# Moving the conv gate columns of a hybrid conv/attention block into the attention stage

## The chip, the core and the metric

The kernel runs on one core of one Trainium2 chip. Time is device microseconds for one execution. Engines are named as in the profile: PE is TensorE (matmuls), PEld its weight loads, DVE is VectorE, ACT is ScalarE, POOL is GpSimd, SP is SyncE, which here only issues DMAs. TensorE's clock is granted at one of two levels, 1.2 or 2.4 GHz; the profile gives it as a share of full speed.

## What is computed

One decoder block on x of 1024 positions by 1024 channels, in fp32:

```
h    = rmsnorm(x, norm_in_g);   P = h @ w_in           # q, 3 x (k, v), branch gates, z_nsa, glu_in, z_conv, merge_g
o    = nsa_attention(...)                              # compressed, selected and window branches, 16 heads
y_nsa  = (o * silu(z_nsa)) @ w_nsa_proj
u    = a * sigmoid(b)                                  # glu_in = (a, b)
c    = silu(layernorm(causal_depthwise_conv31(u), conv_ln_g, conv_ln_b))
y_conv = (c * silu(z_conv)) @ w_conv_proj
g_conv, g_nsa = split(sigmoid(merge_g))
x    = x + (g_conv * y_conv + g_nsa * y_nsa) @ w_out;  out = rmsnorm(x, norm_f_g)
```

## The kernel before

Activations are kept transposed, channels on the 128 partitions and positions along the free axis. A matrix product in fp32 is made of three passes: every operand is split into a high and a low part, and high*high, high*low and low*high are summed in PSUM. `split_w` (line 104) does this for weights: `load_w` brings 4 row blocks of a 128-column strip (256 KB, two `raw` buffers), ScalarE rounds them (`wh`, line 109) and GpSimd takes the rest (`wl`, line 110 through the helper at line 69). A *column* below is one such strip of 128 output channels: 2 halves of 512 positions, 24 matmuls of 512 columns in each half (`mm_seq`, lines 113 to 123), 48 matmuls in all.

The stages, in program order:

- norm of x and transposes; `hT` holds the split h in SBUF, two halves.
- front projections by `project` (line 364): GLU columns, k, q, v. Beside them VectorE runs the depthwise convolution (31 taps, line 347), in pieces that `pump` hands out after each half column. The convolution's result is `cv`, 8 tiles of 128x1024.
- 8 columns of the NSA gate z_nsa (`C_ZN`): ScalarE sigmoid and a VectorE product (`zs`, lines 556, 557), stored to `ZD`.
- the layer norm of `cv` (lines 566 to 599), raised in priority: column sums by matmul with ones, eight subtractions of the mean (line 586), squares, sums on GpSimd (line 590), reciprocal root, eight products (line 594), silu.
- `EARLY` = 3 columns of the merge gates (`C_MG`): one ScalarE tanh each half, stored to `GD`.
- 8 columns of the conv gate z_conv (`C_ZC`, lines 609 to 618): sigmoid, two VectorE products, one of them with the normalised `cv`, stored to `YD`.
- attention in 8 steps of (group, pair of query blocks), order (0,0), (0,1), (1,0), (1,1), (0,2), (0,3), (1,2), (1,3), each with 8 heads. `select` loads q and does the compressed branch, `attend` the other two.
- beside attention, at lowest priority and through one PSUM bank (`fbank`), *filler* matmuls: first the 13 other merge gate columns (`merge_gates`), then the conv projection (`projections`, 8 columns, needs all of `YD`, and uses the memory of `hT`), then most of the NSA projection (`nsa_early`, 8 columns: the first half of positions whole, of the second half 12 matmuls each). `pace` ties the pieces of `nsa_early` to heads of the last two steps, as the earliest point at which they may be issued.
- after attention: the rest of the NSA projection and the output projection.

The order of instructions on each engine is not written by hand. A planner with a cost model simulates the program when it is built, takes the ready instruction with the highest priority and assigns memory; then each engine runs its fixed order. `tc.high_priority(offset=LOW)` pushes work behind everything else. A tile pool that is opened where another was closed may have to wait for that memory. In the kernel before, the pools of attention (`gp` for K, V and bias; `sp` for q; `ap`) are opened after the block that holds `cv`.

Of the kernel before, what the change touches and what calls it, by code (L numbers as in the profile page):

```python
# [16 lines left out]
P = 128  # L17
# [6 lines left out]
HG = 8  # L24
# [30 lines left out]
EARLY = 3  # L55
# [3 lines left out]
def hybrid_block(ctx, tc, x, norm_in_g, w_in, pos_ck, w_ck1, w_ck2, pos_cv, w_cv1, w_cv2,  # L59
# [13 lines left out]
    wp = ctx.enter_context(tc.tile_pool(name="wp", bufs=2))  # L73
    dram = ctx.enter_context(tc.tile_pool(name="dram", bufs=1, space=DRAM))
# [16 lines left out]
    MD = dram.tile([D, S], F32, name="MD")  # L91
    ND = dram.tile([2, D, HALF], F32, name="ND")
# [124 lines left out]

    with ExitStack() as c1:
# [14 lines left out]
        up = c1.enter_context(tc.tile_pool(name="up", bufs=1, reuse_waits="tile"))  # L233
# [90 lines left out]
        pc = c1.enter_context(tc.tile_pool(name="pc", bufs=1, reuse_waits="tile"))  # L324
        pv_ = c1.enter_context(tc.tile_pool(name="pcv", bufs=1, side="right", reuse_waits="tile"))
        st = c1.enter_context(tc.tile_pool(name="st", bufs=2, side="right", reuse_waits="tile"))
        cv = pv_.tile([P, KT, S], F32, name="cv")
        csum = pc.tile([P, S], F32, name="csum")
# [7 lines left out]
        def conv_pair(ct, us):  # L336
            def gen():
                accs = [pcc.tile([P, S], F32, tag="ca", name="ca", bufs=2) for _ in range(2)]
                for k in range(TAPS):
                    for e in range(2):  # L340
                        u, w = us[e][:, k:k + S], vec[:, ct + e, V_CW + k:V_CW + k + 1]
                        if k == 0:
                            nc.vector.tensor_scalar(accs[e], u, w, vec[:, ct + e, V_CB:V_CB + 1],
                                                    op0=ALU.mult, op1=ALU.add)
                        else:
                            dst = accs[e] if k < TAPS - 1 else cv[:, ct + e, :]
                            nc.vector.scalar_tensor_tensor(dst, u, w, accs[e], op0=ALU.mult, op1=ALU.add)  # L347
                        yield
                for e in range(2):
                    if ct + e == 1:  # L350
                        nc.gpsimd.tensor_tensor(csum, cv[:, 0, :], cv[:, 1, :], op=ALU.add)
                    elif ct + e > 1:
                        nc.gpsimd.tensor_tensor(csum, csum, cv[:, ct + e, :], op=ALU.add)
# [17 lines left out]
        def glu_pair(c0):  # L371
            us = []
            for ct in (c0, c0 + 1):
                u, sg = glu_buffers(st) if ct else first_glu
# [171 lines left out]

        nc.gpsimd.memset(bc[:, :, 0:56], 0.0)
        for h4 in range(0, NH, 4):
            tmp = st.tile([P, 4, 256], F32, tag="sg", name="tmp", bufs=2)
# [3 lines left out]
        for t in range(KT):  # L553
            def ev_zn(hf, ps):
                zs = st.tile([P, HALF], F32, tag="zs", name="zs", bufs=2)
# [4 lines left out]
            project(C_ZN + t * P, ev_zn)  # L560
        pump(10 ** 6)
        conv_stack.close()
        psums["ax"] = c1.enter_context(tc.tile_pool(name="pl", bufs=4, space=PSUM, side="right", reuse_waits="tile"))

        lnp = c1.enter_context(tc.tile_pool(name="lnp", bufs=1, reuse_waits="tile"))
        with tc.high_priority(offset=4 * AHEAD):
            mu = lnp.tile([P, S], F32, name="mu")
            def column_sums(total):
# [5 lines left out]
                for hf in range(2):  # L574
                    ps = aux()
# [9 lines left out]
            for k in range(KT):  # L585
                nc.vector.tensor_tensor(cv[:, k, :], cv[:, k, :], mu, op=ALU.subtract)
                sq = lnp.tile([P, S], F32, tag="sq", name="sq", bufs=2) if k else vsum
                nc.scalar.activation(sq, cv[:, k, :], AF.Square)
# [3 lines left out]
            for k in range(KT):  # L592
                sg = st.tile([P, S], F32, tag="sg", name="sg", bufs=2)
                nc.vector.tensor_tensor(cv[:, k, :], cv[:, k, :], rs, op=ALU.mult)
                nc.scalar.activation(sg, cv[:, k, :], AF.Sigmoid, scale=vec[:, k, V_LG:V_LG + 1],
                                     bias=vec[:, k, V_LB:V_LB + 1])
                nc.vector.tensor_scalar(cv[:, k, :], cv[:, k, :], vec[:, k, V_LG:V_LG + 1],
                                        vec[:, k, V_LB:V_LB + 1], op0=ALU.mult, op1=ALU.add)
                nc.gpsimd.tensor_tensor(cv[:, k, :], cv[:, k, :], sg, op=ALU.mult)

        for j in range(EARLY):
            def ev_mg(hf, ps, j=j):
                mg = st.tile([P, HALF], F32, tag="zs", name="mg", bufs=2)
                nc.scalar.activation(mg, ps, AF.Tanh, scale=0.5)
                nc.sync.dma_start(GD[j * P:(j + 1) * P, hf * HALF:(hf + 1) * HALF], mg)

            project(C_MG + j * P, ev_mg)
# [12 lines left out]
    pf = ctx.enter_context(tc.tile_pool(name="pf", bufs=1, space=PSUM, reuse_waits="tile"))  # L620
    ev = ctx.enter_context(tc.tile_pool(name="ev", bufs=3, reuse_waits="tile"))
# [31 lines left out]
    with ExitStack() as c3:  # L653
        psS = c3.enter_context(tc.tile_pool(name="psS", bufs=3, space=PSUM, side="right", reuse_waits="tile"))
        psT = c3.enter_context(tc.tile_pool(name="psT", bufs=3, space=PSUM, reuse_waits="tile"))
        psO = c3.enter_context(tc.tile_pool(name="psO", bufs=1, space=PSUM, reuse_waits="tile"))
        gp = c3.enter_context(tc.tile_pool(name="gp", bufs=1, reuse_waits="tile"))
# [3 lines left out]
        def merge_gates():  # L661
            cols = [w_in[:, C_MG + j * P:C_MG + (j + 1) * P] for j in range(EARLY, 2 * KT)]
            for n, hf, ps in ends_halved(cols, hT, fbank, (False, True)):
                j = EARLY + n
                sl = slice(hf * HALF, (hf + 1) * HALF)
# [3 lines left out]
                nc.sync.dma_start(GD[j * P:(j + 1) * P, sl], mg)  # L669

        with tc.high_priority(offset=LOW):
            merge_gates()

        K = [gp.tile([P, 2, S], F32R, name=f"k{j}") for j in range(2)]
        V = [gp.tile([P, NB, P], F32R, name=f"v{br}") for br in range(2)]
        BT, base, shared = {}, {}, {}

        def load_kv(g, half, slot):
            src_t, dst_t = slice(half * HALF, (half + 1) * HALF), slice(slot * HALF, (slot + 1) * HALF)
            for br in (1, 0):  # L680
                for part in range(2):
                    src = KD[br, part, g * DK:(g + 1) * DK, src_t]
                    for j in range(2):
                        r0 = (part ^ j) * DK
                        nc.sync.dma_start(f(K[j][r0:r0 + DK, br, dst_t]), src)
            for br in (1, 0):
                nc.sync.dma_start(f(V[br][:, 4 * slot:4 * slot + 4, :]),
                                  VD[g, br, src_t].rearrange("(c p) n -> p c n", p=P))
            base[g] = (slot - half) * 4

        def load_bt(g):
            BT[g] = []
            for h8 in range(HG):
# [417 lines left out]
```

## Time and profile before

| | |
|---|---|
| time, median of 3 runs | 1464.44 us (1464.18 to 1464.65) |
| profiled execution, its own time | 1461.95 us |
| its span, first to last instruction | 1460.2 us |
| mean granted TensorE clock | 0.988 |
| matmuls in flight (PE) | 1402.9 us, 96% of the span |
| VectorE busy | 1046.3 us, 72% |
| DMA moved | 171.16 MB |

The profile is one execution. Matmuls are pipelined, so the busy time of PE is the time in which at least one is in flight; it doesn't say how densely they follow each other. Durations of single matmuls overlap for the same reason. The time of an execution is a little longer than its span.

### The profile page before, as it was taken

To read this page: it belongs to the slowest core of one execution; us is meant where nothing else is said; L and a number is where in the kernel's file an instruction comes from. 1 tells how busy PE (TensorE), PEld (TensorE's weight loads), DVE (VectorE), ACT (ScalarE), POOL (GpSimd) and SP (SyncE) were. 2 spreads that over 40 slices of the span, in tenths; PEclk is the share of its full clock that TensorE was granted. 3 is DMA by queue.
4 is the path that set the end of the run, shared out by engine and by line. 5 is a ranking of instruction groups with operands and counts; after the bars stand their busy time and mean duration, and the time that the engine had idled before them with its cause. 6 is when DMAs were issued, how large, how long until landed. Compare 5 with 4: busy or idle time off the path is not lost.

```text
span 1460.2 us, 22837 instructions
## 1 busy us (share of the span) xinstructions
PE 1402.9 (96%) x7516; PEld 1203.8 (82%) x7516; DVE 1046.3 (72%) x2382; ACT 675.7 (46%) x1440; POOL 687.5 (47%) x793
## 2 busy tenths in 40 slices
PE   7999999999989999999999999999999899999997
PEld 6788888888868788778888788898799789898786
DVE  5699999999866522257665956766878988886732
ACT  6331112112144322256666675565567677775422
POOL 2323224233172822255545596455677477774211
PEclk8999999999999999999999999999999999999999
DMA  5243424345223733523333375322444223434732
GB/s 170 70 117 102 129 58 152 109 130 164 80 80 87 197 110 98 148 77 95 91 86 97 94 228 163 95 87 91 155 132 137 78 62 94 152 109 148 216 116 87
DMA packets 185711, 171.16 MB, mean 117 GB/s; under 512 B 12165, under 2 KB 146389, under 8 KB 185592
## 3 DMA queue, kind: packets, MB, share of 16 engines
q1 hardware_dynamic: 183528, 166.55, 38.2%
q10 hardware_dynamic: 2064, 3.15, 0.7%
q8 instruction: 60, 0.98, 0.3%
q14 instruction: 59, 0.48, 0.1%
HBM read 124.01 MB, written 48.78 MB: 118 GB/s over the span
## 4 chain that ended last, share of the span: by engine, by line
PE 80%; DVE 10%; issue 3%; DMA 2%; ACT 2%; POOL 1%; SPq 1%; ACTq 0%; DVEq 0%; POOLq 0%
PE mm L120 10%; PE mm L122 10%; PE mm L121 10%; PE sb L813 6%; PE tb L860 6%; PE fb L120 4%; PE fb L121 3%; PE fb L122 3%; PE ob L886 3%; PE ob L885 3%; PE fb L132 3%; PE fb L133 3%; PE fb L134 3%; PE eb L1044 2%; PE eb L1043 2%
## 5 line engine op out<-in xcount | busy, mean ns | idle before, releaser
L69 POOL TENSOR_TENSOR wl<-raw,wh 128x512 fp32r<-128x512 f32 x184 | 243.6, 1325 | 430.2 <-ACT wh L109 404.1
L120 PE MATMUL mm<-act,wh 128*128 128x512 f32 x720 | 284.5, 395 | 6.8 <-DVE zs L557 6.8
L347 DVE SCALAR_TENSOR_TENSOR ca<-u,vec,ca 128x1024 f32<-128x1024 f32 x232 | 284.0, 1281 | 0.8
L121 PE MATMUL mm<-act,wh 128*128 128x512 f32 x720 | 281.1, 391 | 0.0
L122 PE MATMUL mm<-act,wl 128*128 128x512 f32 x720 | 277.9, 391 | 0.2 <-POOL wl L69 0.2
L109 ACT ACTIVATE wh<-raw 128x512 fp32r<-128x512 f32 x184 | 115.5, 628 | 262.8 <-PE mm L121 179.6
L848 ACT ACTIVATE p<-p,ac 128x640 f32<-128x640 f32 (+7 forms) x256 | 187.5, 734 | 65.2 <-DVE ac L840 55.9
L853 POOL TENSOR_SCALAR p<-p,rcx,gates 128x640 f32<-128x640 f32 (+7 forms) x256 | 200.4, 794 | 10.6
L813 PE MATMUL sb<-k,q 128*128 128x384 f32 (+2 forms) x704 | 178.8, 352 | 6.1 <-DVE ac L840 6.0
L69 DVE TENSOR_TENSOR tl<-tb,th 128x512 fp32r<-128x512 f32 (+1 forms) x272 | 158.4, 591 | 29.5 <-ACT th L864 27.9
L860 PE MATMUL tb<-ident,p 128*128 128x128 f32 x1056 | 169.4, 274 | 5.6 <-DVE tl L69 2.4
L864 ACT ACTIVATE th<-tb 128x512 fp32r<-128x512 f32 (+1 forms) x272 | 136.0, 517 | 68.3 <-PE tb L860 59.2
L120 PEld LDWEIGHTS mm<-act,wh 128*128 128x128 f32 x720 | 135.5, 188 | 36.2 <-DVE zs L557 7.7
L122 PEld LDWEIGHTS mm<-act,wl 128*128 128x128 f32 x720 | 135.6, 188 | 29.3 <-POOL wl L69 0.6
L121 PEld LDWEIGHTS mm<-act,wh 128*128 128x128 f32 x720 | 135.7, 188 | 28.0
L860 PEld LDWEIGHTS tb<-ident,p 128*128 128x128 f32 x1056 | 125.9, 141 | 13.4 <-DVE tl L69 3.1
L813 PEld LDWEIGHTS sb<-k,q 128*128 128x128 f32 x704 | 114.4, 191 | 16.8 <-issue 3.8
L886 PE MATMUL ob<-tl,v 128*128 128x256 f32 x448 | 124.5, 298 | 3.9 <-DVE tl L69 3.4
L885 PE MATMUL ob<-th,v 128*128 128x256 f32 x448 | 124.8, 292 | 0.5 <-ACT th L864 0.4
L120 PE MATMUL fb<-act,wh 128*128 128x512 f32 x240 | 96.3, 401 | 0.7 <-ACT mg L668 0.6
L122 PE MATMUL fb<-act,wl 128*128 128x512 f32 x240 | 95.6, 398 | 0.0
L121 PE MATMUL fb<-act,wh 128*128 128x512 f32 x240 | 95.2, 397 | 0.0
(244 smaller groups left out, 2594.2 us busy)
## 6 DMA issues: line engine op xcount, KB each, us to landing
raw<-in_w_in_dram SPq DMA_DIRECT2D x128, 256.0 KB, 3.0
gt<-GD SPq DMA_DIRECT2D x40, 256.0 KB, 3.2
GD<-mg SPq DMA_DIRECT2D x32, 256.0 KB, 2.8
q<-QD SPq DMA_DIRECT2D x64, 128.0 KB, 3.2
raw<-in_w_nsa_proj_dram SPq DMA_DIRECT2D x32, 256.0 KB, 3.7
raw<-in_w_conv_proj_dram SPq DMA_DIRECT2D x24, 256.0 KB, 3.0
k<-KD SPq DMA_DIRECT2D x40, 128.0 KB, 3.2
xt<-in_x_dram SPq DMA_DIRECT2D x8, 512.0 KB, 6.1
```

Of the source, the lines that this page charges most:

```text
L69: eng.tensor_tensor(low, full, f(high), op=ALU.subtract)
L120: nc.tensor.matmul(ps, wh[:, k, :], mh[:, kk, :], start=(kk == 0), stop=False)
L121: nc.tensor.matmul(ps, wh[:, k, :], ml[:, kk, :], start=False, stop=False)
L122: nc.tensor.matmul(ps, wl[:, k, :], mh[:, kk, :], start=False, stop=(kk == KT - 1))
L347: nc.vector.scalar_tensor_tensor(dst, u, w, accs[e], op0=ALU.mult, op1=ALU.add)
L813: nc.tensor.matmul(s[:, 0:w], lhs, K[j][:, br, k0:k0 + w], start=(j == 0), stop=(j == 1))
L848: nc.scalar.activation(pt[:, 0:n], pt[:, 0:n], AF.Exp, bias=mn, scale=-1.0, accum_out=sm[:, b:b + 1])
L853: nc.gpsimd.tensor_scalar(pt[:, 0:n], pt[:, 0:n], rc[:, b:b + 1], gates[:, 2 * qp + b, gcol:gcol + 1], op0=ALU.mult, op1=ALU.mult)
L860: nc.tensor.transpose(tp[:, j * P:(j + 1) * P], src, ident)
L864: nc.scalar.activation(th, src, AF.Copy)
L885: nc.tensor.matmul(dst, lhs, th[:, sl], start=False, stop=False)
L886: last = nc.tensor.matmul(dst, lhs, tl[:, sl], start=False, stop=False)
```

## The change

Three things. (1) The eight conv gate columns leave the front and become filler in attention, at the head of the filler queue, ahead of the merge gates; `EARLY` goes from 3 to 6, so 10 merge gate columns are left to the filler in place of 13. The normalised conv result is stored to a new DRAM tensor `CD` (8 stores of 512 KB), and each half column of the gate loads its part back (16 loads of 256 KB). silu is computed as tanh with the factor 0.5 folded into the layer norm's scale and bias (`half_ln`), one VectorE instruction in place of two products, and the product with `ct` goes to GpSimd. (2) Ahead of the end of the convolution stand only two NSA gate columns; behind the layer norm come four merge gate columns, then the six other NSA gate columns, and two merge gate columns at lowest priority. (3) The pool of K, V and bias (`gp`) and the PSUM pools of attention are opened ahead of the layer norm, whose column sums use attention's PSUM tiles, and the first loads of K, V and bias are written right behind the layer norm. `cv` becomes eight tiles; the evacuation tiles of the front come from the pool `ev` with three buffers.

```diff
-EARLY = 3
+EARLY = 6
+    ev = ctx.enter_context(tc.tile_pool(name="ev", bufs=3, reuse_waits="tile"))
+    CD = dram.tile([D, S], F32, name="CD")
...
+        half_ln = vp_.tile([P, KT, 2], F32, name="half_ln")
...
-        cv = pv_.tile([P, KT, S], F32, name="cv")
+        cv = [pv_.tile([P, S], F32, name=f"cv{k}") for k in range(KT)]
...
+        nc.vector.tensor_scalar(half_ln, vec[:, :, V_LG:V_LG + 2], 0.5, None, op0=ALU.mult)
...
-        for t in range(KT):
+        def zn_col(t):
             def ev_zn(hf, ps):
-                zs = st.tile([P, HALF], F32, tag="zs", name="zs", bufs=2)
+                zs = ev.tile([P, HALF], F32, tag="ev", name="zs")
...
+        def gate_col(j):
+            def ev_mg(hf, ps):
+                mg = ev.tile([P, HALF], F32, tag="ev", name="mg")
+                nc.scalar.activation(mg, ps, AF.Tanh, scale=0.5)
+                nc.sync.dma_start(GD[j * P:(j + 1) * P, hf * HALF:(hf + 1) * HALF], mg)
+
+            project(C_MG + j * P, ev_mg)
+
+        for t in range(2):
+            zn_col(t)
         pump(10 ** 6)
         conv_stack.close()
-        psums["ax"] = c1.enter_context(tc.tile_pool(name="pl", bufs=4, space=PSUM, side="right", reuse_waits="tile"))
+        up_stack.close()
+        pf = ctx.enter_context(tc.tile_pool(name="pf", bufs=1, space=PSUM, side="right", reuse_waits="tile"))
+        psS = att.enter_context(tc.tile_pool(name="psS", bufs=3, space=PSUM, side="right", reuse_waits="tile"))
+        gp = att.enter_context(tc.tile_pool(name="gp", bufs=1, reuse_waits="tile"))
...
-                    ps = aux()
+                    ps = psS.tile([P, HALF], F32, tag="s", name="sb")
...
+                nc.vector.tensor_scalar(cv[k], cv[k], half_ln[:, k, 0:1], half_ln[:, k, 1:2],
+                                        op0=ALU.mult, op1=ALU.add)
+                nc.gpsimd.tensor_tensor(cv[k], cv[k], sg, op=ALU.mult)
+                nc.sync.dma_start(CD[k * P:(k + 1) * P, :], cv[k])
-        for j in range(EARLY):
...
-        for t in range(KT):
-            def ev_zc(hf, ps):
-                sl = slice(hf * HALF, (hf + 1) * HALF)
-                zs = st.tile([P, HALF], F32, tag="zs", name="zs", bufs=2)
-                nc.scalar.activation(zs, ps, AF.Sigmoid)
-                nc.vector.tensor_tensor(zs, ps, zs, op=ALU.mult)
-                nc.vector.tensor_tensor(zs, zs, cv[:, t, sl], op=ALU.mult)
-                nc.sync.dma_start(YD[t * P:(t + 1) * P, sl], zs)
-
-            project(C_ZC + t * P, ev_zc)
...
+        load_bt(0)
+        load_kv(0, 0, 0)
+        load_kv(1, 0, 1)
+        for j in range(4):
+            gate_col(j)
+        for t in range(2, KT):
+            zn_col(t)
+        with tc.high_priority(offset=LOW):
+            for j in range(4, EARLY):
+                gate_col(j)
...
-        def merge_gates():
...
+        def late_columns():
+            todo = [(C_ZC, t) for t in range(KT)] + [(C_MG, j) for j in range(EARLY, 2 * KT)]
+            cols = [w_in[:, c + j * P:c + (j + 1) * P] for c, j in todo]
+            for n, hf, ps in ends_halved(cols, hT, fbank, (False, True)):
+                kind, j = todo[n]
+                rows_j, sl = slice(j * P, (j + 1) * P), slice(hf * HALF, (hf + 1) * HALF)
+                mg = ev.tile([P, HALF], F32, tag="ev", name="mg")
+                if kind == C_ZC:
+                    ct = ev.tile([P, HALF], F32, tag="ev", name="ct")
+                    nc.sync.dma_start(ct, CD[rows_j, sl])
+                with tc.high_priority(offset=-LOW):
+                    nc.scalar.activation(mg, ps, AF.Tanh, scale=0.5)
+                    if kind == C_ZC:
+                        nc.vector.scalar_tensor_tensor(mg, mg, 1.0, ps, op0=ALU.add, op1=ALU.mult)
+                if kind == C_ZC:
+                    nc.gpsimd.tensor_tensor(mg, mg, ct, op=ALU.mult)
+                    nc.sync.dma_start(YD[rows_j, sl], mg)
+                else:
+                    nc.sync.dma_start(GD[rows_j, sl], mg)
...
-        load_bt(0)
-        load_kv(0, 0, 0)
-        load_kv(1, 0, 1)
         part = select(*steps[0])
```

## Rows read from the trace of the kernel before

**Rows 1.** The page's engine table: busy us, share of the span, instructions.

```profile
PE 1402.9 (96%) x7516; PEld 1203.8 (82%) x7516; DVE 1046.3 (72%) x2382; ACT 675.7 (46%) x1440; POOL 687.5 (47%) x793
```

**Rows 2.** By stretch: PE, PEld, DVE, ACT, POOL busy (instructions), granted clock, DMA share, GB/s.

```profile
50.00:400.00 350.00, 350.00 (x1625) 293.75 (x1625) 330.71 (x313) 71.07 (x135) 105.64 (x86) 1.00 0.40 114
...
650.00:1100.00 450.00, 437.27 (x2609) 385.49 (x2608) 312.62 (x1085) 279.27 (x677) 276.18 (x388) 0.99 0.39 119
...
1200.00:1340.00 140.00, 138.90 (x932) 126.48 (x931) 116.24 (x339) 102.66 (x209) 101.38 (x122) 1.00 0.36 115
```

**Rows 3.** The same view in stretches of 50 us; the first is front projections alone.

```profile
550.00:600.00 50.00, 50.00 (x222) 41.39 (x221) 13.39 (x20) 11.30 (x20) 13.05 (x11) 1.00 0.34 96
1050.00:1100.00 50.00, 50.00 (x309) 44.72 (x308) 32.64 (x99) 29.56 (x59) 38.38 (x45) 1.00 0.48 142
1100.00:1150.00 50.00, 46.76 (x323) 42.63 (x321) 45.40 (x142) 36.54 (x75) 29.66 (x39) 0.97 0.38 110
1150.00:1200.00 50.00, 44.98 (x307) 39.66 (x308) 46.16 (x146) 34.54 (x74) 33.09 (x45) 1.00 0.23 69
```

**Rows 4.** The same view, filler alone (tile fb): PE, PEld, DVE, ACT.

```profile
600.00:850.00 250.00, 154.54 (x592) 107.46 (x590) 0.00 (x0) 14.06 (x24) 0.99 0.36 106
1050.00:1100.00 50.00, 26.62 (x99) 17.21 (x97) 2.71 (x4) 0.00 (x0) 1.00 0.48 142
1100.00:1150.00 50.00, 2.84 (x11) 2.06 (x11) 0.69 (x1) 0.00 (x0) 0.97 0.38 110
1150.00:1200.00 50.00, 6.39 (x24) 4.35 (x24) 0.69 (x1) 0.00 (x0) 1.00 0.23 69
```

**Rows 5.** Layer norm: TensorE's waits (us, times, longest), a stretch, VectorE's timeline.

```profile
PE mm L120 <- DVE zs L557: 6.3, 1, 6.3
...
420.00:440.00 20.00, 13.67 (x53) 10.85 (x53) 11.86 (x7) 7.30 (x9) 18.02 (x8) 0.83 0.23 66
...
411.72 18.25 DVE L586 TENSOR_TENSOR cv<-cv,mu 128x1024 f32<-128x1024 f32 x8 [2.89 <-ACT mu L583]
```

**Rows 6.** Start of attention: TensorE's wait, two stretches, SP's timeline.

```profile
PE sb L718 <- DMA q<-QD: 3.1, 1, 3.1
...
598.00:618.00 20.00, 16.90 (x86) 14.07 (x85) 6.03 (x24) 5.30 (x9) 4.85 (x7) 1.00 0.72 188
618.00:638.00 20.00, 17.47 (x85) 14.28 (x84) 11.93 (x46) 8.78 (x26) 7.39 (x15) 0.91 0.26 82
...
600.48 0.37 SPq L616 DMA_DIRECT2D YD<-zs  x1
600.90 10.41 SPq L704 DMA_DIRECT2D q<-QD  x16
```

**Rows 7.** Timelines of SP (first and last load of bias, K, V) and POOL (norm's end).

```profile
476.89 0.50 SPq L695 DMA_DIRECT2D bt<-TD  x1
...
501.69 1.14 SPq L687 DMA_DIRECT2D v<-VD  x2
...
505.79 2.39 POOL L599 TENSOR_TENSOR cv<-cv,sg 128x1024 f32<-128x1024 f32 x1
```

**Rows 8.** Groups by line and shape: xcount, busy us, mean ns, idle before.

```profile
L69 POOL TENSOR_TENSOR wl<-raw,wh 128x512 fp32r<-128x512 f32 x184 | 243.6, 1325 | 430.2 <-ACT wh L109 404.1 <-PE mm L122 11.0 <-ACT rs L197 8.3
L647 POOL TENSOR_TENSOR gt<-gt,mt 128x512 f32<-128x512 f32 x16 | 20.7, 1292 | 4.5 <-DVE gt L646 3.4 <-DVE rcx L849 1.0
L586 DVE TENSOR_TENSOR cv<-cv,mu 128x1024 f32<-128x1024 f32 x8 | 18.2, 2349 | 2.9 <-ACT mu L583 2.9
L594 DVE TENSOR_TENSOR cv<-cv,ly 128x1024 f32<-128x1024 f32 x8 | 11.4, 1491 | 0.0
L615 DVE TENSOR_TENSOR zs<-zs,cv 128x512 f32<-128x512 f32 x16 | 11.1, 692 | 1.1
```

**Rows 9.** DMA issues by tile: count, KB each, median us to landing.

```profile
mt<-MD SPq DMA_DIRECT2D x16, 256.0 KB, 3.3
ND<-gt SPq DMA_DIRECT2D x16, 256.0 KB, 2.5
```

More of the change, by code (lines that the diff above doesn't have):

```diff
@@ L231, in aux @@
             return psums["ax"].tile([P, HALF], F32, tag="ax", name="ax")
-        up = c1.enter_context(tc.tile_pool(name="up", bufs=1, reuse_waits="tile"))
+        up_stack = ExitStack()
+        up = up_stack.enter_context(tc.tile_pool(name="up", bufs=1, reuse_waits="tile"))
         def glu_buffers(pool):
@@ L373, in glu_pair @@
             for ct in (c0, c0 + 1):
-                u, sg = glu_buffers(st) if ct else first_glu
+                u, sg = glu_buffers(sgp) if ct else first_glu
                 if ct:
@@ L620, in hybrid_block @@
-    pf = ctx.enter_context(tc.tile_pool(name="pf", bufs=1, space=PSUM, reuse_waits="tile"))
-    ev = ctx.enter_context(tc.tile_pool(name="ev", bufs=3, reuse_waits="tile"))
+                nc.vector.tensor_scalar(cv[k], cv[k], half_ln[:, k, 0:1], half_ln[:, k, 1:2],
+                                        op0=ALU.mult, op1=ALU.add)
+                nc.gpsimd.tensor_tensor(cv[k], cv[k], sg, op=ALU.mult)
+                nc.sync.dma_start(CD[k * P:(k + 1) * P, :], cv[k])
+        K = [gp.tile([P, 2, S], F32R, name=f"k{j}") for j in range(2)]
@@ new lines, in hybrid_block, with load_kv @@
+        V = [gp.tile([P, NB, P], F32R, name=f"v{br}") for br in range(2)]
+        BT, base, shared = {}, {}, {}
+        def load_kv(g, half, slot):
+            src_t, dst_t = slice(half * HALF, (half + 1) * HALF), slice(slot * HALF, (slot + 1) * HALF)
+            for br in (1, 0):
+                for part in range(2):
+                    src = KD[br, part, g * DK:(g + 1) * DK, src_t]
+                    for j in range(2):
+                        r0 = (part ^ j) * DK
+                        nc.sync.dma_start(f(K[j][r0:r0 + DK, br, dst_t]), src)
+            for br in (1, 0):
+                nc.sync.dma_start(f(V[br][:, 4 * slot:4 * slot + 4, :]),
+                                  VD[g, br, src_t].rearrange("(c p) n -> p c n", p=P))
+            base[g] = (slot - half) * 4
@@ new lines, in load_bt @@
+        def load_bt(g):
+            BT[g] = []
+            for h8 in range(HG):
+                bt = gp.tile([P, 256], F32, tag="bt", name="bt", bufs=8)
+                nc.sync.dma_start(bt, toeplitz(g * HG + h8))
+                BT[g].append(bt)
+        load_bt(0)
[8 more added lines that the diff above has]
+                gate_col(j)
@@ L651, in hybrid_block @@
     oa = []
-    with ExitStack() as c3:
-        psS = c3.enter_context(tc.tile_pool(name="psS", bufs=3, space=PSUM, side="right", reuse_waits="tile"))
+    with att as c3:
         psT = c3.enter_context(tc.tile_pool(name="psT", bufs=3, space=PSUM, reuse_waits="tile"))
         psO = c3.enter_context(tc.tile_pool(name="psO", bufs=1, space=PSUM, reuse_waits="tile"))
-        gp = c3.enter_context(tc.tile_pool(name="gp", bufs=1, reuse_waits="tile"))
         sp = c3.enter_context(tc.tile_pool(name="sp", bufs=2, reuse_waits="tile"))
@@ L675, in hybrid_block @@
[L675 to L689, printed above, removed]
@@ L691, in load_bt @@
-        def load_bt(g):
-            BT[g] = []
-            for h8 in range(HG):
-                bt = gp.tile([P, 256], F32, tag="bt", name="bt", bufs=8)
-                nc.sync.dma_start(bt, toeplitz(g * HG + h8))
-                BT[g].append(bt)
+                    if kind == C_ZC:
[5 more added lines that the diff above has]
+                    nc.sync.dma_start(GD[rows_j, sl], mg)
```

42 lines of the change are left out of this document (16 added, 26 removed).

## The prediction, made before the change was run

> **What bounds the kernel now.** I read the engine table first [rows 1]: TensorE shows matmuls in 1402.9 of 1460.2 us. The share is an average, so I next took the busy time by stretch [rows 2]. From 50 to 400 us TensorE is busy in all 350.0 us and VectorE in 330.7: projections run beside the convolution and neither has room. From 650 to 1100 us, in attention, TensorE is busy in 437.3 of 450 us and VectorE in only 312.6: TensorE sets the pace, because filler columns are mixed between the attention matmuls. From 1200 to 1340 us TensorE has 138.9 of 140.
>
> So the work of TensorE is the floor, and a change that leaves its matmuls alone can only win where TensorE waits. Three places around the edit show that.
>
> First, the layer norm [rows 5]. TensorE waits 6.3 us, once, for the VectorE evacuation of a NSA gate column (zs, line 557), because VectorE is in an unbroken run of eight subtractions, 18.25 us from 411.72. In 420 to 440 the granted clock is 0.83, so part of that stretch ran at 1.2 instead of 2.4 GHz after the wait: 53 matmuls took 13.67 us, and 53 at the dense rate below are 11.9, so the clock cost another 1.7 us.
>
> Second, the start of attention [rows 6]. TensorE waits 3.1 us for q, and is idle for 20 - 16.90 and 20 - 17.47, together 5.6 us, between 598 and 638, with a granted clock of 0.91 in the second half (0.09 of 20 us, 1.8 us at most). The q loads are issued at 600.90, right behind the store of the last conv gate tile at 600.48.
>
> Third, 1100 to 1200 us [rows 3, 4]. The filler drops from 99 matmuls in 50 us to 11 and 24, VectorE rises to 45.4 and 46.2 of 50, and TensorE is idle for 3.2 + 5.0 = 8.3 us. The hidden slack is larger, since overlapped matmuls still show busy. In 1050 to 1100 nothing is idle: 99 filler matmuls at the dense rate (222 in 50 us, 0.225 us each) are 22.3 us, which leaves 27.7 us for the other 210, 0.132 us each. At that price 1100 to 1150 needs 11 x 0.225 + 312 x 0.132 = 43.7 us and 1150 to 1200 needs 24 x 0.225 + 283 x 0.132 = 42.8. Together 13.5 us of room.
>
> The Trainium skill, Perfetto Trace Analysis, section Identifying the Most-Contended Engine, says that matmul busy time tells little and that the share of weight loading is the better measure of headroom; by it 18% of this kernel would be free, since weight loading is busy for 82%. The trace disagrees: in the dense stretch 550 to 600, with nothing idle, it stands at 41.39 of 50, also 83% [rows 3].
>
> **The change, part by part.** *Columns moved.* Ahead of attention stood 8 NSA gate, 3 merge gate and 8 conv gate columns; now 8 and 6. Five columns of 48 matmuls move into the filler queue, which grows from 13 to 18 columns: 5 x 48 x 0.225 = 54 us leave the front and 54 us enter attention. On TensorE that is zero. It is worth what it puts into idle time, and costs what it leaves over at the end.
>
> *Layer norm.* Only two NSA gate columns now stand ahead of the end of the convolution; while VectorE works through the norm, TensorE has four merge gate columns (43 us), whose evacuation is one ScalarE instruction and needs no VectorE. The 6.3 us wait and its 1.7 us of clock have no cause left. What is late next: the weight splits. GpSimd does them at 1.3 us each [rows 8], the norm's own sums are on it too, and it is busy for 18.0 of 20 us in 420 to 440 [rows 5]. If they are late TensorE waits there instead. Bounds 0 and 8 us; I take 6, because three PSUM banks and three split buffers cover a few us of lateness. The later evacuations of NSA gate columns meet shorter VectorE runs, and before shows no wait there.
>
> *Start of attention.* The tiles of the normalised result no longer live until the last projection, so memory for q frees when the norm ends (its last product on GpSimd starts at 505.79 us [rows 7]) and not at 600; some 30 us of columns then cover the loads and the first selection. Bounds 0 (q still waits) and 5.6 + 1.8 = 7.4; I take 5, since the short dependent chain of the first selection remains.
>
> *K, V and bias in the norm.* The trace has these loads already between 476.89 and 502.83 [rows 7], inside the norm: the planner had moved them. Nothing.
>
> *The conv gate itself.* Two VectorE multiplications per half (0.69 us each) become one, and a GpSimd multiplication of 1.29 us by the nearest row, the same shape in the merge [rows 8]. VectorE loses 16 x 0.69 = 11 us, GpSimd gains 21 us. The half factor goes into constants. Both lie in the first steps of attention, where VectorE has 137 us free of 450 [rows 2]; nothing on the path. If that cover were gone it would cost up to 21 us.
>
> The Trainium skill, SBUF — State Buffer, section SBUF: two separate sides, says that GpSimd and a VectorE instruction with two SBUF inputs lock each other out. That speaks against moving a product to GpSimd. The trace agrees in kind: the same 128x1024 form takes 2349 ns as the subtraction, with GpSimd's sums beside it, and 1491 ns as the later product [rows 8]. By the rule up to 21 us of VectorE would be blocked; by the rows of attention there is room for it.
>
> *The detour through memory.* Eight stores of 512 KB and 16 loads of 256 KB are new, 8 MB in all; the DMA engines are busy for 0.39 in that stage [rows 2]. The load waits for one of three ev buffers, and behind it on the sync queue stand weight and q loads. A half column of 24 matmuls takes about 10 us beside attention (592 filler matmuls in 250 us [rows 4]), a store 2.5 and a load 3.3 [rows 9], so the buffer is back in time. I take 0; if it is not, the wait shows on the sync queue first.
>
> *The gap in attention.* Five more columns push the conv projection 54 us later in filler. At 22.3 us in 50, the rate just before, the 100 us from 1100 would hold 45 us of filler where they hold 35 matmuls, 8 us [rows 4]. That takes 37 of the 54 us; the other 17 go into the 140 us up to 1340, beside what is left there of the merge filler (192 matmuls, 43 us): 60 us in 140, about the share of 1050 to 1100. So it fits. Bounds 0 (the new order leaves another hole) and 13.5; I take 9, near the idle of 8.3 that is plainly visible, since VectorE at 46 of 50 keeps the rest.
>
> *Sum.* -6 - 5 - 9 = -20 us. The profiled execution took 1461.95 us (span 1460.2); minus 20 gives 1442. The median of the three runs lies 2.5 us above the profiled one, so I forecast **1444 us**. The upper bounds together are -28.9, 1435.5 by the median; with only a third of the terms, 1458.
>
> **Rivals.** *A: no change.* All matmuls stay, and a wait comes back elsewhere: weight splits late in the norm (back to 0), the hole in attention moved rather than filled (0), q's gain eaten by its chain. For it: TensorE busy for 96%. Against: the three waits have named causes and the change touches each. 1458 to 1467, 0.17.
>
> *B: slower, by filler left behind attention.* The merge filler (gt and mt loaded, added, stored through three buffers) needs 3.2 + 3.3 + 1.3 + 2.5 = 10.3 us for two buffers of three, so one half per 6.9 us when nothing else runs [rows 8, 9]. Eight of the halves are 12 matmuls, 2.7 us of TensorE: each that spills past the last attention step loses up to 4.2 us. Five spilled halves eat the 20 us; all eight, with the first two gains kept, make 1464 - 11 + 34 = 1487. For it: 54 us more filler in the same attention, and some of the merge tied to late heads. Against: the hole ahead of them, which holds two thirds of the 54 us. 0.12.
>
> *C: the port lock decides.* The 21 us of GpSimd work block VectorE on the path: 1465, 0.05. That is the SBUF page's rule at its worst.
>
> *D: more room.* If the weight loading share of 1200 to 1340 (126.5 of 140, 0.90) could be had in 650 to 1100 (385.5 of 450, 0.86), 20 us more would go: 1424. Against it: filler itself has 0.83. 0.04. That is the Trace Analysis page's reading.
>
> **Numbers.** Forecast 0.62, within 1435 to 1459. Three runs spread over 0.5 us; 0.2% is 2.9 us, about what separates a change from none. Faster: 0.62, D 0.04, a quarter of A 0.04, 0.70 in all. Same: half of A and most of C, 0.13. Slower: B and the rest, 0.17. The range 1432 to 1467 leaves out B, D and the edge of the forecast, about 0.2.
>
> **What would show it.** Right: no TensorE wait for VectorE in the norm and a granted clock of 1.00 there; no wait for q; filler in every 50 us of attention up to its end; the start of attention some 60 us earlier; conv projection ending later against attention. Wrong: GpSimd splits named as TensorE's wait in the norm; a new stretch without filler; merge columns after the last attention step with TensorE waiting for loads; the sync queue waiting for ev buffers while q or weights are late. The planner lays the order out afresh, so a hole at a place that nobody edited is what would most easily make this wrong.

## The result, and the profile after

The changed kernel takes **1430.3 us** (median of 4, 1429.95 to 1432.56) beside 1464.31 for the kernel before on the same chip: ratio 0.9775, interval 0.9758 to 0.9792. That is 34 us where 20 were forecast, and below the range. The span went from 1460.2 to 1428.2 us, 32.0.

The engine table of the page after has the same 7516 matmuls, and 11.9 us less of TensorE's busy time: idle time fell from 57.3 to 37.2 us, so 20.1 of the 32.0 are plain idle time. The rest lies inside time that shows as busy.

```profile
PE 1391.0 (97%) x7516; PEld 1197.0 (84%) x7516; DVE 1032.8 (72%) x2367; ACT 675.4 (47%) x1441; POOL 709.6 (50%) x809
```

To see all of it I cut both traces at the same places: at the first filler matmul, and at each step's last store of the attention output (s0 to s7 are the eight steps; s7 ends with attention's last matmul, and the table ends with the last matmul of all, 7.4 us before the end of the span). From the length of a stretch I took what its matmuls need at the dense rate, start to start: 0.2265 us for 512 columns, 0.176 for 384, 0.139 for 304, 0.1195 for 256, 0.109 to 0.112 for 128, the medians of stretches with nothing idle. What is left is the loss: waits, half clock and thin overlap together. This table is worked out from the traces, in us:

```
            kernel before             kernel after
stretch   length  filler  loss     length  filler  loss   change of loss
0-400      400.0     0    28.7      400.0     0    28.2      -0.5
norm       197.9     0     9.9      133.0     0     2.8      -7.1
s0          95.5   58.0    8.8       86.5   47.1    5.0      -3.8
s1          86.6   42.8    2.4       82.3   39.9    2.4       0.0
s2          54.2   28.1    4.1       53.9   27.6    5.5      +1.4
s3          99.0   45.1    9.4       91.7   46.2    1.8      -7.6
s4         125.3   56.6    7.7      122.8   51.2    9.7      +2.0
s5         108.1   19.5   13.9      133.9   59.1    1.2     -12.7
s6          83.0   19.3    5.2      111.5   49.6    2.2      -3.0
s7          89.8   24.2    2.9       92.6   27.2    3.3      +0.4
tail       113.4     0     4.9      112.7     0     4.0      -0.9
sum                       97.9                     66.0     -31.9
```

("norm" reaches from 400 us to the first filler matmul.) The sum is the difference of the spans to 0.1 us: both kernels have the same matmuls, so what the table does is to say where the difference lies. Five rows carry it: norm, s0, s3, s5 and s6.

The views that answer to [rows 2, 3], after. First a stretch of the norm, the earlier part of attention and its later part; then 50 us at a time where the hole was; columns as in [rows 2].

```profile
420.00:440.00 20.00, 19.83 (x88) 16.00 (x87) 9.64 (x4) 9.00 (x13) 19.84 (x9) 1.00 0.44 123
...
594.00:1044.00 450.00, 441.61 (x2643) 388.95 (x2642) 315.88 (x1095) 278.01 (x658) 267.13 (x370) 0.99 0.35 105
1144.00:1308.00 164.00, 162.84 (x1054) 147.60 (x1053) 122.27 (x351) 109.61 (x219) 122.34 (x139) 1.00 0.43 137
...
1050.00:1100.00 50.00, 50.00 (x307) 44.70 (x306) 42.86 (x121) 26.28 (x55) 24.99 (x33) 1.00 0.47 143
1100.00:1150.00 50.00, 49.32 (x311) 44.05 (x309) 30.93 (x93) 34.99 (x69) 44.25 (x44) 1.00 0.53 170
1150.00:1200.00 50.00, 50.00 (x315) 45.21 (x314) 31.96 (x96) 30.52 (x64) 37.58 (x45) 1.00 0.43 131
```

Filler alone in the same stretches of the kernel after (tile fb, TensorE), against [rows 4]:

```profile
1050.00:1100.00 50.00, 28.88 (x113) 1.00 0.47 143
1100.00:1150.00 50.00, 25.54 (x98) 1.00 0.53 170
1150.00:1200.00 50.00, 25.77 (x100) 1.00 0.43 131
```

The hole is gone: 98 and 100 filler matmuls stand where 11 and 24 stood, the granted clock of 0.97 is 1.00, and TensorE is idle for 0.7 of 100 us instead of 8.3. The 420 to 440 us stretch of the norm now holds 88 matmuls at a clock of 1.00, not 53 at 0.83. TensorE's largest waits in the kernel after, from 400 to 560 us and then in attention (us, times, longest):

```profile
PE mm L122 <- DVE zs L566: 1.3, 1, 1.3
PE sb L835 <- DVE lt L745: 1.0, 1, 1.0
...
PE ob L908 <- DVE tl L69: 3.8, 4, 2.9
PE sb L835 <- DVE ac L862: 1.5, 3, 0.8
```

The 6.3 us for zs [rows 5] is 1.3, and the 3.1 us for q [rows 6] is gone from the start of attention. The queue of SyncE says why for q, and shows one thing that I did not foresee; timeline of the kernel after (start, length, line, transfer, count):

```profile
397.95 1.39 SPq L647 DMA_DIRECT2D bt<-TD  x3
...
418.68 0.92 SPq L639 DMA_DIRECT2D v<-VD  x2
...
469.53 2.10 SPq L726 DMA_DIRECT2D q<-QD  x2
...
477.93 0.54 SPq L624 DMA_DIRECT2D CD<-cv  x1
...
489.85 1.32 SPq L726 DMA_DIRECT2D q<-QD  x2
...
502.12 0.34 SPq L624 DMA_DIRECT2D CD<-cv  x1
...
541.63 0.46 SPq L706 DMA_DIRECT2D ct<-CD  x1
```

The q loads go out from 469.53 on, 63 us ahead of the first filler matmul at 533.0, with the stores of the normalised result among them. Bias, K and V have been issued by 420, some 58 us ahead of that crowd; before they stood between 476.89 and 502.83 [rows 7], where no such stores were.

### The profile page after: what moved, and what is told of

The parts are those of the page before. It is cut to its first block, busy times and chain, and to the rows that moved or that the text cites. A ratio compares the mean times of both kernels' runs of the same rounds, so it can differ in the third digit from the quotient of the medians.

```text
span 1428.2 us, 22832 instructions
## 1 busy us (share of the span) xinstructions
PE 1391.0 (97%) x7516; PEld 1197.0 (84%) x7516; DVE 1032.8 (72%) x2367; ACT 675.4 (47%) x1441; POOL 709.6 (50%) x809
## 4 chain that ended last, share of the span: by engine, by line
PE 82%; DVE 6%; DMA 4%; issue 3%; POOL 3%; ACT 2%; SPq 0%; ACTq 0%; DVEq 0%; POOLq 0%
PE mm L122 9%; PE mm L124 9%; PE mm L123 9%; PE sb L835 7%; PE tb L882 7%; PE fb L122 4%; PE fb L123 4%; PE fb L124 4%; PE ob L908 3%; PE ob L907 3%; PE fb L134 3%; PE fb L135 3%; PE fb L136 3%; PE eb L1063 2%; PE eb L1062 2%
## 5 line engine op out<-in xcount | busy, mean ns | idle before, releaser
L122 PE MATMUL mm<-act,wh 128*128 128x512 f32 x640 | 252.9, 395 | 1.5 <-DVE zs L566 1.3
L123 PE MATMUL mm<-act,wh 128*128 128x512 f32 x640 | 249.6, 390 | 0.0
L124 PE MATMUL mm<-act,wl 128*128 128x512 f32 x640 | 247.2, 390 | 0.0
L882 PE MATMUL tb<-ident,p 128*128 128x128 f32 x1056 | 165.1, 273 | 0.1
L122 PEld LDWEIGHTS mm<-act,wh 128*128 128x128 f32 x640 | 120.1, 188 | 27.6 <-DVE zs L566 1.8
L124 PEld LDWEIGHTS mm<-act,wl 128*128 128x128 f32 x640 | 120.1, 188 | 25.9 <-POOL wl L69 0.6
L123 PEld LDWEIGHTS mm<-act,wh 128*128 128x128 f32 x640 | 120.2, 188 | 24.7
L122 PE MATMUL fb<-act,wh 128*128 128x512 f32 x320 | 127.9, 400 | 2.5 <-ACT mg L708 1.3
L124 PE MATMUL fb<-act,wl 128*128 128x512 f32 x320 | 126.2, 394 | 0.0
L123 PE MATMUL fb<-act,wh 128*128 128x512 f32 x320 | 126.1, 394 | 0.0
L835 PEld LDWEIGHTS sb<-k,q 128*128 128x128 f32 x704 | 114.1, 189 | 12.8 <-DVE ac L862 2.8
```

What stands on the lines that cost most here:

```text
L122: nc.tensor.matmul(ps, wh[:, k, :], mh[:, kk, :], start=(kk == 0), stop=False)
L123: nc.tensor.matmul(ps, wh[:, k, :], ml[:, kk, :], start=False, stop=False)
L124: nc.tensor.matmul(ps, wl[:, k, :], mh[:, kk, :], start=False, stop=(kk == KT - 1))
L835: nc.tensor.matmul(s[:, 0:w], lhs, K[j][:, br, k0:k0 + w], start=(j == 0), stop=(j == 1))
L882: nc.tensor.transpose(tp[:, j * P:(j + 1) * P], src, ident)
```

## The experiments

Theory 1: the change gains because TensorE has work where it waited, and the amount of filler is what counts in attention. Its rivals are named with each run. Ratios are to the kernel before on the same chip; losses are by the table above.

**Filler back to 13 columns.** The changed kernel with five merge gate columns put back ahead of attention (8 conv gate and 5 merge gate columns stay in the filler); all else is as after.

```diff
-EARLY = 6
+EARLY = 11
...
-        for j in range(4):
+        for j in range(EARLY - 2):
             gate_col(j)
...
-            for j in range(4, EARLY):
+            for j in range(EARLY - 2, EARLY):
```

> The changed kernel with EARLY = 11: five merge gate columns go back to the front, so the filler queue again has 13 columns (8 conv gates, 5 merge gates), while the new order around the layer norm, the early pools and the store and reload of the conv result stay. Theory 1 (the amount of filler pays: attention had room that the old queue could not fill): the layer norm's 7 us and the 4 us at the start of attention stay, the rest of the gain goes, so about 1453 us, 20 to 24 above the changed kernel, with a stretch of attention that has little filler. Rival (the new order and memory layout pay, the amount does not matter): 1436 or less.

1448.70 us, ratio 0.9905 (0.9883 to 0.9927), against 0.9775: by the ratios 19 us of the gain are gone with five columns, 3.8 us each, and about 14 us stay. The hole is back in the same place (a window of 50 us; below it filler alone):

```profile
1100.00:1150.00 50.00, 44.41 (x290) 38.76 (x289) 41.77 (x122) 32.34 (x67) 26.07 (x35) 0.97 0.43 127
```

```profile
1100.00:1150.00 50.00, 6.23 (x24) 0.97 0.43 127
1150.00:1200.00 50.00, 12.44 (x48) 1.00 0.25 75
```

Losses: norm 1.2, s3 11.4, s5 14.9, s6 5.2. So norm is repaired without the filler, and s3, s5 and s6 are not.

**The order around the norm alone.** The kernel before, with two NSA gate columns ahead of the norm, the merge gates in it and the other six behind it.

```diff
-        for t in range(KT):
+        def zn_col(t):
...
+        for t in range(2):
+            zn_col(t)
         pump(10 ** 6)
...
             project(C_MG + j * P, ev_mg)
+        for t in range(2, KT):
+            zn_col(t)
```

> The kernel before with the order around the layer norm alone changed: two NSA gate columns, the norm, three merge gate columns, six NSA gate columns, then the conv gates as before. The filler queue is that of before. Theory 1: the 6.3 us wait for VectorE in the norm and its clock loss go, nothing else moves: 1457 us (1455 to 1459), the start of attention and the thin stretch as before. Rival (the wait comes back as late weight splits): 1463 to 1465.

1453.29 us, ratio 0.9935 (0.991 to 0.996): 7.6 us by the medians, 9.5 by the ratio, whose interval is 6 to 13 us. The loss of norm falls from 9.9 to 2.2, s5 and s6 stay at 12.8 and 5.2. The wait on TensorE is named zs still, and is short; q's is as it was:

```profile
PE sb L724 <- DMA q<-QD: 3.0, 1, 3.0
PE mm L120 <- DVE zs L557: 0.5, 1, 0.5
```

The order is the whole of the norm's term. s0 loses 10.6 here, against 5.0 in the run before this one, which has 13 columns of filler too, and the early memory, the early loads, the conv gate as filler and the detour. No run has the early memory alone, so that q's wait went because of it is read from the queue above and not shown by itself.

**The same filler spread another way.** The rival: the hole comes from the pacing of the NSA filler, not from its amount. The kernel before, with the pacing list changed.

```diff
-        turns = [-1] * 4 + [1, 3, 5, 7] + list(range(7, 15))
+        turns = [-1] * 8 + list(range(7, 15))
```

> The kernel before with the pacing of the NSA projection's early halves loosened: eight halves free at once in place of four, the other eight tied as before. Theory 1 (filler is short in sum): the hole between 1107 and 1185 us is filled, but the two last steps have as much less, and VectorE sets their pace: 1459 to 1464. Rival (the hole alone was the loss, because of the pacing): 12 us or more gained, 1452 or less.

1466.51 us, ratio 1.003 (1.0017 to 1.0042). The hole moved by 50 to 100 us and was not filled (filler alone, then all of TensorE's row):

```profile
1100.00:1150.00 50.00, 24.25 (x93) 1.00 0.48 142
1150.00:1200.00 50.00, 4.27 (x16) 0.97 0.48 151
1200.00:1250.00 50.00, 0.00 (x0) 1.00 0.07 22
```

```profile
1150.00:1200.00 50.00, 40.60 (x251) 32.67 (x249) 46.62 (x124) 31.78 (x61) 26.39 (x33) 0.97 0.48 151
```

Loss of s6 10.3 instead of 5.2, s5 14.7. The pacing falls as a cause; the amount stands.

**More filler: 20, 21 and 22 columns.** The changed kernel with fewer merge gate columns ahead of attention. The question is where rival B, filler left behind, begins.

```diff
-EARLY = 6
+EARLY = 4
```

For 22 columns (21 likewise, with 3):

```diff
-EARLY = 6
+EARLY = 2
...
-        for j in range(4):
+        for j in range(2):
             gate_col(j)
...
-            for j in range(4, EARLY):
+            for j in range(2, EARLY):
```

> The changed kernel with EARLY = 4: two more merge gate columns leave the front, 20 columns in the filler queue. Theory 1 with the room used up (2 to 3 us of loss left in each of the last steps): 1427 to 1432, no clear difference. Rival (more room still): 1424 or less, some 4 us per column as in the change. Rival (spill): merge halves behind the last attention step, 1438 or more.

> The changed kernel with EARLY = 3: 21 columns in the filler queue, between 20 (0.9726 of before) and 22 (0.9918, with the merge halves behind the last attention step waiting 15.3 us for their gate tiles). Theory 1 (free room is worth some 4 us a column, a column too many spills about four merge halves of which each waits 3 to 5 us): 0.973 to 0.980, with some filler behind the last attention step. Rival (21 columns still fit): 0.970 or below.

> The changed kernel with EARLY = 2: 22 columns in the filler queue, only two merge gate columns behind the norm. With EARLY = 4 it was 0.9726 of before, against 0.9775 with 6, some 3.6 us per column. Theory 1 (room in attention that filler can take): the last steps still took 40 us of filler with 2 us of loss, so again up to 7 us: 0.968 to 0.972. Rival (room used up, merge halves spill behind attention): 0.975 or above. Rival (two gate columns, 22 us, no longer cover the 18 us run of VectorE in the norm, with the wait for it back): 0.973 to 0.977 and a TensorE wait of some 5 us before 450 us.

```
columns of filler   13       18       20       21       22
ratio to before     0.9905   0.9775   0.9726   0.9834   0.9918
filler behind
attention, us        0        0        0       10.9     16.3
loss of tail         3.4      4.0      3.7      9.7     23.8
loss in all         83.9     66.0     58.2     68.9     86.8
```

(Chips differ between some columns of this table, hence ratios.) With 20 columns the kernel takes 1422.39 us, ratio 0.9726 (0.9701 to 0.975), the fastest version found, by the ratios 3.6 us for each of the two columns more. Its s4 and s5 lose 1.8 and 1.0 us. With 21 it turns round (the profiled execution took 1432.94 us against a median of 1436.44, so the losses in its column are at the low end). What the filler behind attention costs shows in the run with 22, where attention's last matmul is at 1293 us and the last filler at 1341; a window, and TensorE's and SyncE's waits from 1200 to 1345:

```profile
1295.00:1345.00 50.00, 36.02 (x126) 27.65 (x125) 17.02 (x18) 15.28 (x19) 24.64 (x17) 0.83 0.85 281
```

```profile
PE fb L134 <- DVE gt L684: 15.3, 5, 5.6
...
SPq L680 <- DMA ND<-gt: 28.9, 13, 5.7
```

TensorE is idle for 14 of 50 us, the granted clock is 0.83, and the wait goes TensorE, VectorE's addition, SyncE's load, the store that holds one of the three buffers. That is rival B's chain as the prediction laid it out. 16.3 us of filler are six halves of 12 matmuls (2.7 us each), and tail loses 23.8 - 4.0 = 19.8 us more than after: 3.3 us for a half, near the 4.2 that the prediction gave as the most. It begins at 21 columns; the 18 of the change fit, as the forecast had it against rival B. The spill is not the whole of what 22 columns lose: norm loses 4.7 us and s0 8.5, against 2.7 and 4.3 with 20. The third rival's wait before 450 us isn't there (TensorE's longest for zs is 0.5 us), but TensorE waits 2.9 us for VectorE's `lt` at the start of attention, and from 497 to 517 us the clock is 0.83.

**Bias, K and V loaded late.** The changed kernel with these loads and their pool back at attention's start. My prediction has them at nothing.

```diff
-        load_bt(0)
-        load_kv(0, 0, 0)
-        load_kv(1, 0, 1)
         for j in range(4):
...
         steps = [(0, 0), (0, 1), (1, 0), (1, 1), (0, 2), (0, 3), (1, 2), (1, 3)]
+        load_bt(0)
+        load_kv(0, 0, 0)
+        load_kv(1, 0, 1)
```

> The changed kernel with the pool of K, V and bias opened again with attention, and their first loads written ahead of the first selection as in the kernel before. Theory 1 (the early loads pay nothing, since the loads of before landed inside the norm as well, 476.89 to 502.83): within 2 us of the changed kernel, 0.976 to 0.979 of before. Rival (they carry part of the gain at the start of attention): 4 us or more slower, 0.980 or above.

1436.42 us, ratio 0.9813 (0.9789 to 0.9836): by the ratios 5 to 6 us slower than after, with intervals that overlap a little; the trace, of an execution of 1439.09 us, shows a place. The loads are issued between 474.56 and 507, among the eight stores of the normalised result; norm loses 6.6 us, s0 6.6, together 5.4 more than after. Two stretches there, TensorE's wait for a split from 400 to 620 us, and ScalarE's wait for weights from 470 to 520:

```profile
480.00:500.00 20.00, 17.14 (x75) 13.39 (x73) 16.06 (x21) 11.94 (x14) 16.15 (x9) 0.99 1.00 318
500.00:520.00 20.00, 20.00 (x84) 16.47 (x85) 2.96 (x6) 4.21 (x7) 8.05 (x6) 0.92 0.78 258
```

```profile
PE mm L122 <- ACT wh L111: 1.3, 2, 1.1
...
ACT wh L111 <- DMA raw<-in_w_in_dram: 5.7, 3, 2.4
```

The DMA engines are busy for 1.00 of the first stretch, weights come late, TensorE waits for their split, and the clock is 0.92 in the stretch behind it. After, the DMA engines are nearly as busy in 480 to 500 (0.96), but TensorE is busy for all 20.00 us and the clock is 1.00 in both stretches. So a cost of the late loads is likely, and its size of some 5 us is not certain.

**The detour left out.** The changed kernel without the stores of the normalised result, their loads and the product on GpSimd.

```diff
-                nc.sync.dma_start(CD[k * P:(k + 1) * P, :], cv[k])
...
-                    ct = ev.tile([P, HALF], F32, tag="ev", name="ct")
-                    nc.sync.dma_start(ct, CD[rows_j, sl])
...
-                    nc.gpsimd.tensor_tensor(mg, mg, ct, op=ALU.mult)
```

> The changed kernel without the store of the conv result, without its 16 reloads and without the GpSimd product with it; the conv gate alone goes into the conv projection, so the conv result is left out. Theory 1 (the detour costs nothing): within 2 us of the changed kernel, 0.976 to 0.979 of before. Rival (the reloads and the 21 us of GpSimd products hold attention up): 4 us or more faster, 0.975 or below.

1427.72 us, ratio 0.9753 (0.9728 to 0.9779), against 0.9775: about 3 us faster, between the two theories, with intervals that overlap. If 8 MB of traffic and 21 us of GpSimd cost anything, it is about that.

**The conv gate product on VectorE.** The changed kernel with that product moved from GpSimd.

```diff
-                    nc.gpsimd.tensor_tensor(mg, mg, ct, op=ALU.mult)
+                    nc.vector.tensor_tensor(mg, mg, ct, op=ALU.mult)
```

> The changed kernel with the product of the conv gate and the conv result on VectorE in place of GpSimd (16 of 0.69 us against 16 of 1.30). Theory 1 (neither engine is on the path there): 0.976 to 0.979, as the changed kernel. Rival (GpSimd's products hold VectorE or attention up): 0.974 or below. Rival (VectorE's 11 us count): 0.982 or above.

1434.57 us, ratio 0.9818 (0.9792 to 0.9845), with single times from 1431.71 to 1437.94. If anything it is slower than after; the intervals touch, and it stands between theory 1 and the rival by which VectorE's 11 us count. Rival C, by which GpSimd's product blocks VectorE on the path, wanted it faster, and falls.

**The loss that is left in s4.** After, 9.7 us are lost in s4, around the handover to the conv projection, whose input ya is loaded and split there. Ten us of it in a window, and the timeline in it of GpSimd (first two rows) and VectorE (last two):

```profile
940.00:950.00 10.00, 6.05 (x23) 4.59 (x22) 9.96 (x20) 4.45 (x9) 10.00 (x6) 0.69 0.37 127
```

```profile
940.77 2.58 POOL L69 TENSOR_TENSOR act<-act 128x1024 fp32r<-128x1024 f32 x1
944.79 4.68 POOL L69 TENSOR_TENSOR act<-act 128x1024 fp32r<-128x1024 f32 x2
...
941.46 2.24 DVE L767 SCALAR_TENSOR_TENSOR lt<-lt 128x312 f32<-128x312 f32 x1
945.26 1.91 DVE L752 TENSOR_SCALAR sm<-sm 128x8 f32<-128x8 f32 x1
```

Theory 2: GpSimd's split of ya stretches VectorE's selection, and TensorE waits for that. Two runs: the split moved to VectorE, and the split cut to a short piece.

```diff
-  load_half((ya[0][hf], ya[1][hf]), YD[:, hf * HALF:(hf + 1) * HALF], range(4), nc.gpsimd, AHEAD)
+  load_half((ya[0][hf], ya[1][hf]), YD[:, hf * HALF:(hf + 1) * HALF], range(4), nc.vector, AHEAD)
```

> The changed kernel with the low parts of the conv projection's input taken on VectorE in place of GpSimd (8 instructions of 128x1024, GpSimd 2.4 us each). Theory 2 (in 940 to 950 us of the changed kernel GpSimd is busy for 10.0 of 10 us with them, and small VectorE instructions with SBUF inputs stretch to 1.9 and 2.2 us, which ends in a TensorE wait of 2.9 us and 6.8 us at the lower clock): those waits go, 4 to 6 us faster, 0.973 to 0.975 of before. Rival (the loads of the handover are late, whatever engine splits them): no change. Rival (VectorE, which now has 8 x 1.3 us more, becomes late itself): 2 us or more slower.

```diff
-  load_half((ya[0][hf], ya[1][hf]), YD[:, hf * HALF:(hf + 1) * HALF], range(4), nc.gpsimd, AHEAD)
+  load_half((ya[0][hf], ya[1][hf]), YD[:, hf * HALF:(hf + 1) * HALF], range(4), nc.gpsimd, AHEAD, 32)
...
+                if cut:
+                    l, h = l[:, :, 0:cut], h[:, :, 0:cut]
                 sub_low(eng, l, f(l), h)
```

> The changed kernel with GpSimd's low parts of the conv projection's input cut to the first 32 of 512 columns, so the product is not exact; loads, roundings and order stay. Theory 2 (the long GpSimd instructions stretch VectorE's small ones beside them in 940 to 950 us): no VectorE instruction there above 1.5 us where it took 0.4 to 1.0 elsewhere, the TensorE wait of 2.9 us and the fall of the clock go, 5 to 7 us faster than the changed kernel, 0.972 to 0.974. Rival (the stretch is bound by VectorE's own chain of the next selection and by the input loads): the clock falls as before, 0.976 to 0.979.

On VectorE: 1441.97 us, ratio 0.985 (0.9829 to 0.987), 11 us slower than after, with 10.5 lost in s4 and 10.1 in s5. Cut short: 1427.66 us, ratio 0.9769 (0.9746 to 0.9791), no clear difference from after. In the latter GpSimd is light and no VectorE instruction from 925 to 952 us takes over 1.0 us; but s4 still loses 8.3, some of it 10 us later:

```profile
940.00:950.00 10.00, 9.32 (x46) 7.53 (x47) 9.94 (x29) 5.43 (x12) 4.21 (x5) 1.00 0.41 133
950.00:960.00 10.00, 7.88 (x39) 6.25 (x39) 9.94 (x36) 5.19 (x11) 7.14 (x11) 0.84 0.27 79
```

VectorE is busy for 9.94 of 10 us in both. So the stretching is real and at most a small part of the loss. VectorE's own selection beside the handover is what is left; with 20 columns, where the handover meets the selection elsewhere, s4 loses 1.8. That was not tried by itself.

## Why the prediction was wrong

The sign, the mechanism and the three places were right; the size of one place was not, and a fourth was missed.

- **Layer norm, -6.** Measured -7.1 in the table, and -7.7 there by the order alone. Right, and the cause is shown: no other edit was in that run. GpSimd's splits, named as late next, were not: no TensorE wait of the norm after names them, and 0.2 us names ScalarE's part.
- **Start of attention, -5.** Measured -3.8, since s0 keeps 5.0 us. q's wait is gone, as forecast. The two runs with 13 columns differ by 10.6 - 5.0 = 5.6 us there, in more than the memory for q. Right within its bounds.
- **The gap in attention, -9, bounds 0 and 13.5. This is the step that failed.** s5 and s6, which hold the gap, lose 15.7 us less, above the upper bound. The bound priced every matmul of 1100 to 1200 us that is not filler at 0.132 us, the mean of 1050 to 1100. That mean belongs to another mix of shapes (20 of its 210 matmuls have 512 columns, against 24 of 310 and 8 of 282 in the two halves of the hole): by the price of each shape, those of 1100 to 1150 need 0.128 us on average and those of 1150 to 1200 0.124, and the loss there is 7.8 + 9.7 = 17.5 us. That stood in the trace of before. The choice of 9 went by the idle time on view, because VectorE at 46 of 50 was to keep the rest. It did not: of the 15.7 us, 7.7 were idle time and the other 8.0 lay inside time that shows as busy. With filler there VectorE is busy for 30.93 and 31.96 of 50, since less of the attention work falls into the same time. The run with 13 columns prices a column at 3.8 us, 19 for the five, s3 included; the forecast had 9 / 5 = 1.8.
- **No term for the rest of attention.** s3 gains 7.6 us and s4 loses 2.0. Before, ya is loaded and split during s3, and the clock is at half for 3.4 us at 902 us; after, filler that is ahead of it in the queue pushes this into s4. The run with 13 columns splits ya in s3 again (845 to 885 us) and has 11.4 lost there, so it is the five columns that move the loss; that the handover itself makes it is argued, not shown. I had looked for waits around the edit alone.
- **The clock.** Leaving out the first 50 us and the last 10, the kernel before runs at half clock in five stretches (6.8 us and four times 3.4, 20.5 in all), the one after in one (6.8). Half of the difference, 6.9 us at most, is gain that no wait shows; it is inside the losses above, not beside them. My sum had 1.7 for one of them and at most 1.8 for another.
- **K, V and bias: nothing.** Compared with before they gain nothing, as forecast; but with the new stores on the same queue they would have cost some 5 us by the medians had they stayed, which the forecast didn't see. The intervals don't settle it.
- **The conv gate and the detour: nothing.** Right within 3 us by the medians, and no better than the intervals tell.
- **A reading.** The 2349 ns of the subtraction, taken as with GpSimd's sums beside it, is a mean over eight [rows 8]: three that begin inside a sum take 3.36 to 3.42 us, three that end before the first sum begins 1.21 to 1.58. The 1491 ns of the later product are six of 1.21 to 1.22 us and two of 2.31 beside a weight split. The kind of effect is right, the pairing of the two means isn't.
- **Rivals.** A: the waits that came back (s4's) are small. B: its chain is shown, from 21 columns on, three more than the change has. C fell. D, more room (1424, 0.04), was the nearest in size and had the wrong place: weight loading from 594 to 1044 us is busy for 388.95 of 450, 0.86 as before [rows 2], and not 0.90. The gain came from 1100 to 1200, where it rose from 82.29 of 100 [rows 3] to 89.26, and from s3.

What stays open: what holds s4's 9.7 us, and why the split on VectorE loses 10 us in s5 as well (the clock is at half there from 1113.7 us on, for 10.2 us).

## What to carry to other kernels

When filler runs out before the stage that it covers, price a column by running with more and with fewer: here each was worth 3.6 to 3.8 us up to 20 columns, and the idle time on view said half of that. Stop one column before the first filler is left behind the stage, because there the short end of the queue runs at the speed of its buffers. Loads that wait for nothing are better placed ahead of a crowd on their queue, even if they look hidden where they are; here that was worth some 5 us by the medians.

## What the runs showed of the hardware

Some short VectorE instructions beside a long GpSimd one end with it. In the timeline above the 128x8 instruction begins at 945.26 and takes 1.91 us, against a median of 0.168 over its 16; it ends at 947.17, as the first of the two GpSimd instructions does (944.79 + 2.34 = 947.13). The 128x312 one takes 2.24 us beside a GpSimd instruction that ends at 943.35, 0.35 us ahead of its own end at 943.70. The Trainium skill, SBUF — State Buffer, section SBUF: two separate sides, has the shared port, for VectorE instructions with two inputs in SBUF or in a two-port mode, as an exclusive lock that is held for the whole instruction, not a split of bandwidth; these two agree with that, though no run shows the mode of the 128x8 one, which has a single input. It cost the kernel nothing that the run with the short split could show.

Which instructions are hit depends on the form. Of the 128x16 products and sums `im` with `cs` (both inputs in SBUF) and the 128x8 `sm`, all that begin in a GpSimd instruction of over 1 us which runs on 0.3 us past their usual end are stretched, 7 of 7 before and 4 of 4 after, and end 0.03 to 0.04 us behind it; the reciprocals `rc` (128x8) and reductions `im<-ih` that begin so keep their usual 0.19 to 0.21 us, 6 of 6 before and 3 of 3 after. The layer norm of the kernel before shows the same on large tiles: GpSimd's sums end at 420.06, 423.40 and 426.68 us, and VectorE's three subtractions beside them 1.08 to 1.09 us later, at 421.15, 424.49 and 427.77.

Half clock (1.2 GHz) came in stretches of 3.4 or 6.8 us inside attention, and not only beside long waits. In the kernel before it began at 632.1, 901.8, 1045.2 and 1137.3 us; the longest idle time of TensorE in the ten us ahead of each was 1.1, 1.8, 3.6 and 0.5 us. In the kernel after, TensorE waits 2.9 us for tl, which VectorE writes from 944.66 to 945.33, and the clock is at half from 943.8, inside that wait, for 6.8 us. With 20 columns no such stretch is left between 50 and 1410 us.
